# Output projection of a hybrid decoder layer from seven products per 2x2 by 2x2 tiles, with two weight sums made by accumulating DMAs

## The chip, the cores and the metric

One Trainium2 chip, one of its cores. The metric is the device time of one execution in microseconds (us); lower is better. The kernel before took 2497.19 us, the median of 3 runs (2496.21 to 2499.42).

## The reference, cut to what matters

One layer of a decoder trunk on 256 tokens of width 4096: a gated linear attention and a sliding-window attention side by side, gated and merged, one output projection with a residual add, and a final norm. All data are float32.

```python
h = rms_norm(x, norm_gains)
z = h @ w_in                       # 4096 x 19472, split into the parts below
o_a = rms_norm(gla_mix(gq, gk, gv, log_a), gla_norm_gains)
y_a = (o_a * silu(gg)) @ w_gla_out
o_b = swa_sink_mix(sq, sk, sv, sinks)
y_b = (o_b * silu(sg)) @ w_swa_out
merged = sigmoid(ga + b_gates[0]) * y_a + sigmoid(gb + b_gates[1]) * y_b
x = x + merged @ w_out             # 256 x 4096 by 4096 x 4096: what the change is about
out = rms_norm(x, final_norm_gain)
```

## The kernel before

All large projections go through one helper, `gemm` (L125). It makes 512 columns of output for both tiles of 128 tokens, over k tiles of 128 rows. A chunk of two k tiles of weights (128 x 1024, 512 KB) is loaded into `raw` (four buffers), and split in two parts in the format fp32r: ScalarE casts it to `hi` (L154), VectorE subtracts this from `raw` to get `lo` (L155). Each pair of tiles then takes three products, high by high, high by low and low by high (L136 to L138), which add up in one bank of PSUM. The split tiles have three buffers (`STG`). The loads and the split stand in a `tc.high_priority(PRIO)` block, so they are put ahead of other work of their engines.

The program is written with a tile framework: a tile of a pool has as many buffers as `bufs` says, per tag. A new tile of the tag waits until the last reader of the tile that held the buffer is done. The framework orders the instructions of each engine ahead of time from their priorities and from when they could start, so neighbours in the code can change places; each engine then runs its own list in order.

The stages follow one another: the input's norm, the linear attention (two groups of four heads), the window attention, then for each of eight blocks of 512 columns the two gates `ga` and `gb` and the projection `yb` with the merge into `ya` (L502 to L524), and last the output projection. For this the merged activations are transposed and split into `mT` by `transpose_split` (L179), called from `merged` (L499): the first seven blocks before the last `yb` products, the eighth inside the first block of the output projection. The output projection (L530 to L548) then calls `gemm` for each of eight blocks with `wout`, adds the residual (L545), takes squares for the final norm (L546) and multiplies by the gain (L548). In the last block the second token tile's products come late, so that the first tile's final norm lies beside them. At the end each token tile is scaled and stored in five pieces (L549 to L563).

Of the kernel before, what the change touches and what calls it, by code (L numbers as in the profile page):

```python
# [8 lines left out]
F32 = mybir.dt.float32  # L9
# [5 lines left out]
P = 128  # L15
S = 256
# [30 lines left out]
def trunk_kernel(  # L47
# [20 lines left out]
    big = ctx.enter_context(tc.tile_pool(name="big", bufs=1))  # L68
    stage = ctx.enter_context(tc.tile_pool(name="stage", bufs=STG))
    acc_ps = ctx.enter_context(tc.tile_pool(name="acc_ps", bufs=4, space=bass.MemoryType.PSUM))  # L70
    ps = ctx.enter_context(tc.tile_pool(name="ps", bufs=4, space=bass.MemoryType.PSUM))
# [25 lines left out]
    def first_inputs(gp, ssq):  # L97
        """Loads the input as the first block needs it; its squares add up in ssq."""
# [72 lines left out]
    def split_to(dst, src_ps):  # L171
        """dst[:, ..hi/lo.., :] from a PSUM tile of the same layout less the hi/lo axis."""
# [4 lines left out]
    def transpose_split(oT, kt0, src, nk, name):  # L177
        """src [tokens, t, nk*128] -> oT[:, kt0:kt0+nk, hi/lo, tokens]"""
# [12 lines left out]
    # ================= gated linear attention =================  # L191
    with tc.tile_pool(name="gla", bufs=1) as gp:
# [5 lines left out]
        # per-token scale of the input norm  # L198
# [8 lines left out]
        # low-rank decay input, transposed: rows 0-15 from w's high part, 16-31 from its low part  # L207
# [31 lines left out]
        def headsT(name, acc, scale):  # L239
            """[tokens, 4 heads x 128] in PSUM -> [128, head, token]"""  # L240
# [20 lines left out]
        for g in range(2):  # L261
# [3 lines left out]
            # log decays of the group's heads and their running sums in each chunk  # L265
# [51 lines left out]
            # keys of chunks 0 and 1 as chunks 2 and 3 see them  # L317
# [8 lines left out]
            for p in range(2):  # L326
# [6 lines left out]
                # o = A @ v, a head at a time; A is kept transposed, [key, query]  # L333
# [57 lines left out]
    # ================= sliding-window attention =================  # L391
    late = ctx.enter_context(tc.tile_pool(name="late", bufs=1))
# [105 lines left out]
    # ================= gates and merge =================  # L498
    def merged(n):  # L499
        transpose_split(mT, n * 4, ya[:, :, n * NB : (n + 1) * NB], 4, f"m{n}")  # L500

    with tc.tile_pool(name="mrg", bufs=1) as mp:  # L502
        for n in range(NBLK):
# [22 lines left out]
    # ================= output projection, residual, final norm =================  # L526
    with tc.tile_pool(name="fin", bufs=1) as fp:
        gf = fp.tile([P, DM], F32, name="gf")
        nc.scalar.dma_start(gf, gfin.partition_broadcast(P))
        hold = None  # L530
        x2 = big.tile([P, NT, DM], F32, tag="oT", name="x2")
        st = fp.tile([P, NT, NBLK], F32, name="st")
        for n in range(NBLK):
            cs = slice(n * NB, (n + 1) * NB)
            xt = fp.tile([P, NT, NB], F32, tag="xt", name=f"xt{n}", bufs=2)
            nc.scalar.dma_start(xt, x[:, cs].rearrange("(t p) c -> p t c", p=P))
            if n == NBLK - 1:
                hold = late.tile([P, 4, 2, KW, NB], F32R, tag="ya", name="hold")
# [89 lines left out]
```

## Time and profile before

| What | Value |
|---|---|
| median of 3 runs | 2497.19 us |
| span of the profiled execution | 2494.7 us |
| TensorE (PE) busy | 2469.9 us, 99% |
| VectorE (DVE) busy | 1306.1 us, 52% |
| ScalarE (ACT) busy | 1093.1 us, 44% |
| GpSimd (POOL) busy | 41.4 us, 2% |
| moved by DMA | 474.32 MB, 190 GB/s on average |

The profile is of one execution; its own device time is not on the page apart from the span, which reaches from its first to its last instruction. The median of the runs lies 2.5 us above the span. PE is matrix products, PEld their weight loads, SP the engine that issues the weight loads from HBM. "Idle before, releaser" tells what ended an engine's wait.

### The profile page before, as it was taken

The numbers are of one execution on the slowest core, as the hardware profiler recorded it, in microseconds if no ns is written. First come the engines' busy times: TensorE is split into PE (matmuls) and PEld (weight loads), VectorE is DVE, ScalarE is ACT, GpSimd is POOL, SyncE is SP. The second block draws the span as 40 slices with busy tenths as digits, with TensorE's granted clock in tenths as the row PEclk, the third lists the DMA queues.
The fourth block names the chain that finished last, engine by engine and source line by source line (L and its number), as shares of the span: only waits on it lengthen the run. The fifth ranks groups of instructions, "written<-read, shape, count | busy, mean of one in ns | idle before, by whom it ended". The sixth has DMA issues, their size and how long they took to land.

```text
span 2494.7 us, 28744 instructions
## 1 busy us (share of the span) xinstructions
PE 2469.9 (99%) x11220; PEld 2033.3 (82%) x11220; DVE 1306.1 (52%) x1303; ACT 1093.1 (44%) x1289; POOL 41.4 (2%) x52
## 2 busy tenths in 40 slices
PE   8999999999999999999999999999999999999998
PEld 6788888888888888888888888888888888888886
DVE  8565555545444455555555454555545456544544
ACT  6444444434444444544444444444444444444443
POOL 4000000000000000000000000000000000000000
PEclk9999999999999999999999999999999999999999
DMA  7455555445555545454465556665666555665655
GB/s 258 156 175 188 170 175 195 175 168 188 194 192 195 193 148 193 150 171 166 150 211 199 198 198 197 197 202 197 198 196 198 194 194 177 236 211 203 211 203 186
DMA packets 132985, 474.32 MB, mean 190 GB/s; under 512 B 15056, under 2 KB 15440, under 8 KB 132720
## 3 DMA queue, kind: packets, MB, share of 16 engines
q1 hardware_dynamic: 127584, 461.69, 54.5%
q10 hardware_dynamic: 5264, 10.79, 1.4%
q8 instruction: 88, 1.44, 0.2%
q14 instruction: 49, 0.40, 0.0%
HBM read 468.23 MB, written 4.19 MB: 189 GB/s over the span
## 4 chain that ended last, share of the span: by engine, by line
PE 95%; DVE 2%; issue 1%; ACT 1%; DMA 0%; POOL 0%; SPq 0%; ACTq 0%; POOLq 0%; DVEq 0%
PE ga_a L137 5%; PE ga_a L136 5%; PE gb_a L137 5%; PE gb_a L136 5%; PE ga_a L138 5%; PE gb_a L138 5%; PE o_a L136 5%; PE o_a L137 5%; PE o_a L138 5%; PE sg_a L137 2%; PE sg_a L136 2%; PE sg_a L138 2%; PE sq_a L138 2%; PE sq_a L137 2%; PE ya_a L136 2%; PE ya_a L137 2%
## 5 line engine op out<-in xcount | busy, mean ns | idle before, releaser
L155 DVE TENSOR_TENSOR ga_l<-ga_r,ga_h 128x1024 fp32r<-128x1024 f32 x128 | 156.8, 1225 | 171.6 <-ACT ga_h L154 171.6
L155 DVE TENSOR_TENSOR gb_l<-gb_r,gb_h 128x1024 fp32r<-128x1024 f32 x128 | 156.9, 1225 | 171.1 <-ACT gb_h L154 171.1
L155 DVE TENSOR_TENSOR o_l<-o_r,o_h 128x1024 fp32r<-128x1024 f32 x124 | 152.0, 1225 | 161.4 <-ACT o_h L154 161.3
L154 ACT CAST ga_h<-ga_r 128x1024 fp32r<-128x1024 f32 x128 | 135.2, 1057 | 209.8 <-PE ga_a L138 171.5
L154 ACT CAST gb_h<-gb_r 128x1024 fp32r<-128x1024 f32 x128 | 135.2, 1056 | 204.5 <-PE gb_a L138 159.4
L154 ACT CAST o_h<-o_r 128x1024 fp32r<-128x1024 f32 x124 | 131.0, 1056 | 193.2 <-PE o_a L138 186.2
L138 PE MATMUL ga_a<-ga_h,hT 128*128 128x512 f32 x512 | 199.4, 389 | 0.0
L137 PE MATMUL ga_a<-ga_l,hT 128*128 128x512 f32 x512 | 199.2, 389 | 0.0
L136 PE MATMUL ga_a<-ga_h,hT 128*128 128x512 f32 x512 | 199.2, 389 | 0.0
L138 PE MATMUL gb_a<-gb_h,hT 128*128 128x512 f32 x512 | 199.2, 389 | 0.0
L136 PE MATMUL gb_a<-gb_h,hT 128*128 128x512 f32 x512 | 199.2, 389 | 0.0
L137 PE MATMUL gb_a<-gb_l,hT 128*128 128x512 f32 x512 | 199.2, 389 | 0.0
L138 PE MATMUL o_a<-o_h,mT 128*128 128x512 f32 x496 | 193.0, 389 | 0.0
L137 PE MATMUL o_a<-o_l,mT 128*128 128x512 f32 x496 | 193.0, 389 | 0.0
L136 PE MATMUL o_a<-o_h,mT 128*128 128x512 f32 x496 | 192.9, 389 | 0.0
L155 DVE TENSOR_TENSOR ya_l<-ya_r,ya_h 128x1024 fp32r<-128x1024 f32 x64 | 78.4, 1226 | 95.6 <-ACT ya_h L154 95.6
L155 DVE TENSOR_TENSOR sq_l<-sq_r,sq_h 128x1024 fp32r<-128x1024 f32 x64 | 78.4, 1225 | 84.8 <-ACT sq_h L154 84.8
L155 DVE TENSOR_TENSOR yb_l<-yb_r,yb_h 128x1024 fp32r<-128x1024 f32 x64 | 78.4, 1225 | 82.8 <-ACT yb_h L154 82.8
L155 DVE TENSOR_TENSOR gg_l<-gg_r,gg_h 128x1024 fp32r<-128x1024 f32 x64 | 78.3, 1224 | 75.9 <-ACT gg_h L154 75.9
L155 DVE TENSOR_TENSOR sg_l<-sg_r,sg_h 128x1024 fp32r<-128x1024 f32 x64 | 78.3, 1223 | 72.7 <-ACT sg_h L154 72.7
L154 ACT CAST sg_h<-sg_r 128x1024 fp32r<-128x1024 f32 x64 | 67.4, 1053 | 111.0 <-PE sg_a L138 94.7
L155 DVE TENSOR_TENSOR gv_l<-gv_r,gv_h 128x1024 fp32r<-128x1024 f32 x64 | 78.2, 1224 | 67.9 <-ACT gv_h L154 67.9
(278 smaller groups left out, 5568.3 us busy)
## 6 DMA issues: line engine op xcount, KB each, us to landing
ga_r<-in_win_dram SPq DMA_DIRECT2D x128, 512.0 KB, 4.3
gb_r<-in_win_dram SPq DMA_DIRECT2D x128, 512.0 KB, 4.2
o_r<-in_wout_dram SPq DMA_DIRECT2D x128, 512.0 KB, 3.3
gv_r<-in_win_dram SPq DMA_DIRECT2D x64, 512.0 KB, 3.2
gg_r<-in_win_dram SPq DMA_DIRECT2D x64, 512.0 KB, 3.3
ya_r<-in_wgla_dram SPq DMA_DIRECT2D x64, 512.0 KB, 3.2
sq_r<-in_win_dram SPq DMA_DIRECT2D x64, 512.0 KB, 3.2
sg_r<-in_win_dram SPq DMA_DIRECT2D x64, 512.0 KB, 3.3
```

The source lines that it names most:

```text
L136: nc.tensor.matmul(acc[t], lh, hi[:, i, :], start=kt == 0, stop=False)
L137: nc.tensor.matmul(acc[t], lh, lo[:, i, :], start=False, stop=False)
L138: nc.tensor.matmul(acc[t], ll, hi[:, i, :], start=False, stop=kt == nkt - 1)
L154: nc.scalar.copy(hi, raw)
L155: nc.vector.tensor_tensor(lo, raw, hi.bitcast(F32), ALU.subtract)
```

## The change

The output projection no longer goes through `gemm`. Its 2 token tiles, 2 k tiles and 2 column blocks at a time are multiplied with seven products in place of eight, from sums and differences of the tiles (the Winograd form of Strassen's scheme). The left-hand sums are made once by `combine`, for 16 pairs of k tiles. The weights come as four tiles of 128 x 512 in one load of 1 MB (`raw`, two buffers); the host lays them out in that order (`_quads`). Two products take their weight tile and their activations as plain float32 (`right[1]`, `right[2]`). The other five are split as before, one of them from a weight tile itself and four from sums. Two of these sums, `t13`, are made by VectorE in one instruction; the third and the fourth come from adding `raw[:, 0]` and then `raw[:, 3]` into `t13[:, 1]` in place, by DMAs that GpSimd issues with `accum_op`. The split tiles have one buffer each. Seven PSUM banks hold the seven products over all 16 steps, and eight operations then put the four output blocks together from them (`u`, `v`, `y`, `w`). The pools of the earlier stages are closed before this stage, and the new pools take their place; each tile in them waits for what used its own place. `gfin` is loaded in pieces of 1024 columns, and the last block's late second half with `hold` is gone; the stores are four pieces of 1024 columns for each token tile.

```diff
+NFULL = 2
+T13 = 3
+BUFS = {"b": 1, "13": 1, "2": 1, "4": 1}
...
-            if n == NBLK - 1:
-                mT = big.tile([P, KT, 2, S], F32R, tag="hT", name="mT")
-                for m in range(n):
-                    merged(m)
...
+    early.close()
+    NPR = KT // 2
...
+    def combine(j):
+
+        fl, sp_ = full[j // GRP][:, j % GRP], split[j // GRP][:, j % GRP]
+        tp = qps.tile([P, 512], F32, tag="tp", name=f"m_t{j}")
+        for k in range(2):
             for t in range(NT):
...
+                c = (2 * j + k) * P
+                nc.tensor.transpose(tp[:, k * S + t * P : k * S + (t + 1) * P], ya[:, t, c : c + P], ident)
+        tv = tp.rearrange("p (k t c) -> p k t c", k=2, t=NT)
+        cs = fp.tile([P, 6, P], F32, tag="cs", name=f"cs{j}", bufs=2)
+        nc.scalar.copy(fl[:, 0:2, :], tv[:, :, 0, :])
+        nc.scalar.copy(cs[:, 0:2, :], tv[:, :, 1, :])
+        s4 = fl[:, 2, :] if NFULL > 2 else cs[:, 5, :]
+        nc.vector.tensor_tensor(cs[:, 2, :], cs[:, 0, :], cs[:, 1, :], ALU.subtract)
+        nc.vector.tensor_tensor(cs[:, 4, :], fl[:, 0, :], cs[:, 0, :], ALU.subtract)
+        nc.vector.tensor_tensor(cs[:, 3, :], cs[:, 2, :], fl[:, 0, :], ALU.subtract)
+        nc.vector.tensor_tensor(s4, fl[:, 1, :], cs[:, 3, :], ALU.add)
+        c = cs[:, 1 : 8 - NFULL, :]
+        nc.scalar.copy(sp_[:, :, 0, :], c)
+        nc.vector.tensor_tensor(sp_[:, :, 1, :], c, sp_[:, :, 0, :].bitcast(F32), ALU.subtract)
...
+    def sevens(name, w, npr):
+
+        q = {i: qps.tile([P, NB], F32, tag=f"q{i}", name=f"{name}_q{i}") for i in range(1, 8)}
+        for j in range(npr):
+            with tc.high_priority(PRIO):
+                raw = wp.tile([P, 4, NB], F32, tag="raw", name=f"{name}_r{j}", bufs=2)
+                nc.sync.dma_start(raw, w[j])
+                t13 = wp.tile([P, 2, NB], F32, tag="t13", name=f"{name}_t{j}", bufs=T13)
+                nc.vector.tensor_tensor(
+                    t13, raw[:, 0:2, :], raw[:, 2:3, :].broadcast_to([P, 2, NB]), ALU.add
+                )
+
+                def parts(tag, src, n):
+                    hi = wp.tile([P, n, NB], F32R, tag=f"h{tag}", name=f"{name}_h{tag}_{j}", bufs=BUFS[tag])
+                    lo = wp.tile([P, n, NB], F32R, tag=f"l{tag}", name=f"{name}_l{tag}_{j}", bufs=BUFS[tag])
+                    nc.scalar.copy(hi, src)
+                    nc.vector.tensor_tensor(lo, src, hi.bitcast(F32), ALU.subtract)
+                    return [(hi[:, i, :], lo[:, i, :]) for i in range(n)]
+
+                right = {1: raw[:, 0, :], 2: raw[:, 3, :]}
...
+                    right[3], = parts("b", raw[:, 1:2, :], 1)
+                right[5], right[7] = parts("13", t13, 2)
+                t = t13[:, 1, :]
+                nc.gpsimd.dma_start(t, raw[:, 0, :], accum_op=ALU.add)
+                right[6], = parts("2", t13[:, 1:2, :], 1)
+                nc.gpsimd.dma_start(t, raw[:, 3, :], accum_op=ALU.add)
+                right[4], = parts("4", t13[:, 1:2, :], 1)
+            order = (1, 6, 5, 3, 2, 7, 4) if j == npr - 1 else (1, 2, 3, 5, 7, 6, 4)
+            st, sp_ = j == 0, j == npr - 1
+            for i in order:
+                if isinstance(right[i], tuple):
+                    l = split[j // GRP][:, j % GRP, SPLIT[i]]
+                    hi, lo = right[i]
+                    nc.tensor.matmul(q[i], l[:, 0, :], hi, start=st, stop=False)
+                    nc.tensor.matmul(q[i], l[:, 0, :], lo, start=False, stop=False)
+                    nc.tensor.matmul(q[i], l[:, 1, :], hi, start=False, stop=sp_)
+                else:
+                    nc.tensor.matmul(q[i], full[j // GRP][:, j % GRP, FULL[i], :], right[i], start=st, stop=sp_)
+        return q
...
+    for j in range(NPR):
+        combine(j)
+    for n in range(0, NBLK, 2):
...
+        q = sevens(f"o{n}", wout[n // 2], NPR)
...
+        def done(t, i):
+            o, xi = x2[:, t, cs[i]], xt[:, t, i * NB : (i + 1) * NB]
+            add(o, o, xi)
+            nc.scalar.activation(xi, o, AF.Square, accum_out=st[:, t, n + i : n + i + 1])
+            add(o, o, gf_[:, i * NB : (i + 1) * NB], ALU.mult)
+
+        nc.scalar.copy(u, q[1])
+        add(v, q[6], u)
+        add(y, q[5], v, ALU.subtract)
+        add(x2[:, 0, cs[1]], q[3], y)
+        add(x2[:, 0, cs[0]], q[2], u)
+        add(w, q[7], v)
+        add(x2[:, 1, cs[1]], q[5], w, ALU.subtract)
+        add(x2[:, 1, cs[0]], q[4], w)
+        for t, i in ((0, 1), (0, 0), (1, 1), (1, 0)):
+            done(t, i)
```

## Rows read from the trace of the kernel before

**Rows 1.** The page: busy time by engine, and the chain that ended last.
```profile
PE 2469.9 (99%) x11220; PEld 2033.3 (82%) x11220; DVE 1306.1 (52%) x1303; ACT 1093.1 (44%) x1289; POOL 41.4 (2%) x52
...
PE 95%; DVE 2%; issue 1%; ACT 1%; DMA 0%; POOL 0%; SPq 0%; ACTq 0%; POOLq 0%; DVEq 0%
```

**Rows 2.** Busy time by engine in one stretch, the output projection; clock, DMA share, GB/s.
```profile
2134.50:2484.00 349.50, 349.50 (x1546) 289.13 (x1545) 177.44 (x167) 145.42 (x160) 0.55 (x1) 1.00 0.60 208
```

**Rows 3.** Waits from 2140 to 2484 us: us in total, times, longest.
```profile
ACT o_h L154 <- PE o_a L138: 184.5, 116, 2.1
...
ACT o_h L154 <- DMA o_r<-in_wout_dram: 1.6, 3, 0.9
```

**Rows 4.** Timeline of PE near 2300 us: start, duration, engine, line.
```profile
2299.81 0.39 PE L137 MATMUL o_a<-o_l,mT 128*128 128x512 f32 x1
...
2300.49 0.39 PE L137 MATMUL o_a<-o_l,mT 128*128 128x512 f32 x1
```

**Rows 5.** Timeline at the stage's start and at its end.
```profile
2127.90 1.23 DVE L155 TENSOR_TENSOR yb_l<-yb_r,yb_h 128x1024 fp32r<-128x1024 f32 x1 [1.49 <-ACT yb_h L154]
...
2134.48 1.28 DVE L523 TENSOR_TENSOR sgm<-yb_a,sgm 128x512 f32<-128x512 f32 x2
...
2484.06 0.69 DVE L545 TENSOR_TENSOR x<-o_a,xt 128x512 f32<-128x512 f32 x1 [4.98 <-PE o_a L138]
```

**Rows 6.** Timeline of PE, plain float32 products of 256 columns.
```profile
262.41 0.59 PE L366 MATMUL op<-v,ats 128*128 128x256 f32 x2
262.84 0.59 PE L367 MATMUL op<-v,ats 128*128 128x256 f32 x2
```

**Rows 7.** VectorE by line and shape: busy us, mean ns of one.
```profile
L155 DVE TENSOR_TENSOR o_l<-o_r,o_h 128x1024 fp32r<-128x1024 f32 x124 | 152.0, 1225 | 161.4 <-ACT o_h L154 161.3
...
L388 DVE TENSOR_TENSOR gt<-oraw,gt 128x256 f32<-128x256 f32 x16 | 6.2, 420 | 0.2
...
L155 DVE TENSOR_TENSOR gq_l<-gq_r,gq_h 128x512 fp32r<-128x512 f32 x2 | 1.4, 689 | 1.1 <-ACT gq_h L154 1.1
...
L456 DVE TENSOR_TENSOR mx<-mx,sink_sb 128x8 f32<-128x8 f32 x8 | 1.3, 163 | 0.1
```

**Rows 8.** ScalarE by line and shape.
```profile
L154 ACT CAST o_h<-o_r 128x1024 fp32r<-128x1024 f32 x124 | 131.0, 1056 | 193.2 <-PE o_a L138 186.2 <-PE yb_a L138 5.0 <-DMA o_r<-in_wout_dram 1.6
...
L154 ACT CAST gq_h<-gq_r 128x512 fp32r<-128x512 f32 x2 | 1.2, 618 | 0.9 <-DMA gq_r<-in_win_dram 0.9
```

**Rows 9.** DMA issues: count, KB each, median us to landing.
```profile
o_r<-in_wout_dram SPq DMA_DIRECT2D x128, 512.0 KB, 3.3
...
xsb<-in_xT_dram SPq DMA_DIRECT2D x7, 512.0 KB, 6.7
...
gf<-in_gfin_dram ACTq DMA_DIRECT2D x1, 2048.0 KB, 8.1
```

**Rows 10.** The tile `bt`, 256 KB from HBM: 16 loads.
```profile
DMA to landing us min/median/max: 3.9/4.6/6.4
```

**Rows 11.** The output's stores out of SBUF, 256 or 512 KB: 10 stores.
```profile
DMA to landing us min/median/max: 2.1/3.9/4.8
```

**Rows 12.** Timeline of PE: transposes that stand earlier in the code between `yb` products.
```profile
2109.65 0.39 PE L136 MATMUL yb_a<-yb_h,obT 128*128 128x512 f32 x1
...
2110.08 0.66 PE L184 MATMUL m_t<-ident,ya 128*128 128x128 f32 x4
...
2110.49 0.48 PE L137 MATMUL yb_a<-yb_l,obT 128*128 128x512 f32 x1
```

**Rows 13.** Busy time by engine after the last product; the clock stands after POOL's.
```profile
2484.00:2494.70 10.70, 0.02 (x1) 0.00 (x0) 2.82 (x6) 2.91 (x4) 0.56 (x1) 0.63 0.57 223
```

More of the change, by code (lines that the diff above doesn't have):

```diff
@@ L67, in trunk_kernel @@
     const = ctx.enter_context(tc.tile_pool(name="const", bufs=1))
[L68 to L71, printed above, removed]
+    early = ExitStack()
+    big = early.enter_context(tc.tile_pool(name="big", bufs=1))
+    stage = early.enter_context(tc.tile_pool(name="stage", bufs=STG))
+    acc_ps = early.enter_context(tc.tile_pool(name="acc_ps", bufs=4, space=bass.MemoryType.PSUM))
+    ps = early.enter_context(tc.tile_pool(name="ps", bufs=4, space=bass.MemoryType.PSUM))
     def pst(name):
@@ L389, in trunk_kernel @@
                 transpose_split(oaT, pi * 4, gt, 4, f"oa{pi}")
-    late = ctx.enter_context(tc.tile_pool(name="late", bufs=1))
+    late = ctx.enter_context(tc.tile_pool(name="late", bufs=1, side="right"))
     ya = late.tile([P, NT, DM], F32, tag="ya", name="ya")
@@ new lines, in trunk_kernel @@
+    early.close()
+    NPR = KT // 2
+    hp = ctx.enter_context(tc.tile_pool(name="hp", bufs=1, reuse_waits="tile"))
+    wp = ctx.enter_context(tc.tile_pool(name="wp", bufs=1, reuse_waits="tile"))
+    fp = ctx.enter_context(tc.tile_pool(name="fp", bufs=1, reuse_waits="tile"))
+    qps = ctx.enter_context(
+        tc.tile_pool(name="qps", bufs=1, space=bass.MemoryType.PSUM, reuse_waits="tile")
+    )
+    GRP = 4
+    full = [hp.tile([P, GRP, NFULL, P], F32, name=f"full{g}") for g in range(NPR // GRP)]
@@ new lines, in trunk_kernel @@
+    split = [hp.tile([P, GRP, 7 - NFULL, 2, P], F32R, name=f"split{g}") for g in range(NPR // GRP)]
+    def combine(j):
+        fl, sp_ = full[j // GRP][:, j % GRP], split[j // GRP][:, j % GRP]
+        tp = qps.tile([P, 512], F32, tag="tp", name=f"m_t{j}")
+        for k in range(2):
+            for t in range(NT):
+                c = (2 * j + k) * P
[12 more added lines that the diff above has]
+        nc.vector.tensor_tensor(sp_[:, :, 1, :], c, sp_[:, :, 0, :].bitcast(F32), ALU.subtract)
@@ new lines, in trunk_kernel, with add @@
+    x2 = late.tile([P, NT, DM], F32, tag="ya", name="x2")
+    st = fp.tile([P, NT, NBLK], F32, name="st")
+    for j in range(NPR):
+        combine(j)
+    for n in range(0, NBLK, 2):
+        gf_ = fp.tile([P, 2 * NB], F32, tag="gf", name=f"gf{n}")
+        nc.scalar.dma_start(gf_, gfin[n * NB : (n + 2) * NB].partition_broadcast(P))
+        xt = fp.tile([P, NT, 2 * NB], F32, tag="xt", name=f"xt{n}")
+        nc.scalar.dma_start(xt, x[:, n * NB : (n + 2) * NB].rearrange("(t p) c -> p t c", p=P))
+        q = sevens(f"o{n}", wout[n // 2], NPR)
+        cs = [slice((n + i) * NB, (n + i + 1) * NB) for i in range(2)]
+        u = fp.tile([P, NB], F32, tag="u", name=f"u{n}")
+        v = fp.tile([P, NB], F32, tag="v", name=f"v{n}")
+        y = fp.tile([P, NB], F32, tag="y", name=f"y{n}")
+        w = fp.tile([P, NB], F32, tag="w", name=f"w{n}")
+        def add(o, a, b, op=ALU.add):
+            nc.vector.tensor_tensor(o, a, b, op)
+        def done(t, i):
[13 more added lines that the diff above has]
+            done(t, i)
@@ new lines, in trunk_kernel @@
+    for t in range(NT):
+        sf = fp.tile([P, 1], F32, name=f"sf{t}")
+        nc.vector.tensor_reduce(sf, st[:, t, :], AX.X, ALU.add)
+        rms_scale(sf, sf, DM)
+        for c in range(4):
+            os = slice(c * 1024, (c + 1) * 1024)
+            if c % 2 == 0:
+                nc.vector.tensor_scalar(x2[:, t, os], x2[:, t, os], sf, None, ALU.mult)
+            else:
+                nc.scalar.activation(x2[:, t, os], x2[:, t, os], AF.Copy, scale=sf)
+            nc.sync.dma_start(out[t * P : (t + 1) * P, os], x2[:, t, os])
@@ L572, in _tiles, with _quads @@
     return np.ascontiguousarray(w.transpose(3, 0, 2, 1, 4))
+def _quads(w, nblk):
+    import numpy as np
+    w = w.reshape(w.shape[0] // (2 * P), 2, P, nblk // 2, 2, NB)
+    return np.stack([w[:, k, :, :, n] for k, n in ((0, 0), (1, 1), (0, 1), (1, 0))], 3).transpose(2, 0, 1, 3, 4).copy()
 def kernel(**inputs):
```

44 lines of the change are left out of this document (6 added, 38 removed).

## The prediction

> **What bounds the kernel now.** I read the page first. TensorE (PE) is busy 99% of the span and carries 95% of the chain that ended last, the DMA 0% [rows 1]. So what the change is worth has to be read in the stage that it rewrites. The output projection runs from the end of the last `yb` products at 2134.5 us to 2484 us; the table by stretches shows PE busy in all 349.5 us of it, VectorE (DVE) in 177 and ScalarE (ACT) in 145, at the full granted clock, with the DMA engines 60% busy [rows 2]. The waits of the same stretch say who waits for whom: the split of the weights waits for PE to give a staging buffer back (184.5 us), and for its own data from HBM only 1.6 us [rows 3]. The weights are thus always ready before PE asks for them. Between two starts of the same line lie 0.68 us for three products of 512 columns, 0.227 us each [rows 4]; the 1536 of the stage give 348 us. After the last product comes a tail of 10.6 us: add, squares, scale, store [rows 5].
>
> The span is 2494.7 us; the median of the runs, 2497.19, lies 2.5 us above it. I count in the span and add 2.5.
>
> **What PE gains.** For each pair of k tiles and pair of column blocks there are now 8 products in three parts, 24 x 0.227 = 5.44 us. After, there are 7: five in three parts and two as plain float32. The trace has plain float32 products in the attention parts: each is recorded as two instructions, and for 256 columns the next pair starts 0.43 us later [rows 6]. At 512 columns that is twice as much, 0.86 us (lower bound 0.43, if most of it were a fixed cost; no row suggests more than double). One step is 15 x 0.227 + 2 x 0.86 = 5.12 us, and 64 steps (4 pairs of column blocks x 16 pairs of k tiles) are 328 us: PE itself gains 20 us.
>
> **What the other engines get.** Durations of DVE: 1.225 us for 1024 columns, 0.689 for 512, 0.42 for 256, 0.163 for nearly nothing; ACT casts: 1.056 and 0.618 [rows 7, 8]. A step asks of DVE the pair of sums `t13` (1.225), the low part of `t13` (1.225) and three low parts of 512 (2.07): 4.52 us, against 2.45 for the two chunks that it replaces. ACT has 1.056 + 3 x 0.618 = 2.91 us. At each of four column pairs DVE has 15 adds and multiplies of 512 columns, 10.3 us. The 16 `combine` calls have four subtractions of 128 columns (about 0.28 each, between the 0.163 and the 0.42) and one of 640 (about 0.82), 1.94 us, so 31 us. DVE's sum is 289 + 41 + 31 = 361 us: more than the 349.5 us that the stage takes today, before any wait is counted.
>
> **The new chain, and why it decides.** One weight tile `raw` (1 MB) has two buffers. Its last reader is the second accumulating DMA, which adds `raw[:,3]` into the running sum. The steps ahead of that stand in one line, because each rewrites what the one before had to read: load; `t13` sum; cast and low part of `t13` (both must have read it); first accumulate into it; cast and low part of that ("2"); second accumulate. Only then may the load of the step after next start. Before, a raw buffer was free as soon as DVE had made the low part, and there were four.
>
> Priced: the load is 1 MB. Loads of 512 KB land 3.3 us after issue, the one of 2048 KB 8.1 [rows 9]; 1.6 per 512 KB gives 4.9. Then 1.225 + 1.056 + 1.225, and 0.618 + 0.689 for "2". Without the accumulates the chain is 9.71 us. An accumulate X within SBUF, issued from GpSimd (POOL), is in no row. It moves 256 KB as 128 rows of 2 KB; the nearest row has that size and shape, the load `bt`, which lands after 3.9 to 6.4 us with a median of 4.6 beside weight loads [rows 10]. That is a read from HBM and no addition. Bound below: the quickest store, out of SBUF, took 2.1 us [rows 11]. Bound above: 6.4, the slowest `bt`. It can cost nothing only if nothing waited for it, which the chain excludes. I take 4.6. The chain is 9.71 + 9.2 = 18.9 us, and with two buffers two steps pass in it: 9.46 us a step against PE's 5.12. For 64 steps that is 605 us. With 2.1 us it would be 13.9 us a pair and 445 us; with 6.4, 22.5 and 720.
>
> The Trainium skill (page "DMA: Bandwidth & Descriptors", section "Anatomy of one DMA — SWDGE (gpsimd) path") fits a DMA issued from GpSimd as 2.0 us plus bytes over 436 GB/s. By that an accumulate would take 2.6 us (an estimate from the page), the chain 14.9 us and the 64 steps 477 us. The `bt` row is nearly twice that figure for the same bytes. No run here shows an accumulate yet.
>
> A second loop runs beside the first, because the split tiles `h13`, `l13`, `h2`, `l2`, `h4`, `l4` have one buffer each. If PE keeps the order of the code, product 7 of a step must end before the next `t13` cast starts, and product 4 of that next step is the last link before further products: 1.06 + 1.23 + X + 1.31 + X + 1.31 + 0.7 + 3.8 (the products of the following step up to 7) = 9.4 + 2X for two steps, 18.6 us. It is as long as the first, so mixing up PE's order would not help much. The order need not be kept: today transposes from earlier in the code stand between later products where their buffers were late [rows 12].
>
> **Queues.** POOL has no other work in the stage (0.55 us, rows 2) and issues both accumulates of a step in one queue; a waiting one holds back only accumulates behind it. On DVE the low part of "2" waits for an accumulate, and sums, low parts of the next step and the adds of a column pair may stand behind it; what that costs lies within the two buffers' slack of one DVE instruction or two, and I count nothing for it in the middle, up to 3.7 us a pair of steps at the top of the range. SP issues only the weight loads, and each waits for the second accumulate of two steps back; nothing but the stores at the end is behind them.
>
> **Start, boundaries, end.** The first load can go where the last `yb` chunk has left the staging area, at about 2129.1 us, the end of the row at 2127.90 [rows 5]. The second chain trails the first by 3.6 us, since its `t13` cast waits for product 7 (8.4 + 1.36 - 6.1). The `combine` calls today lie under the `yb` products; now they wait for the freed PSUM banks and stand in the first 31 us of the stage. In a step of 9.46 us their 1.94 us are covered; if the chain were short, they would cost up to 31. At the three inner boundaries DVE's 10.3 us come on top of its 9.0 in a period of 18.9: I count 2 us each (0 to 10). Evacuation of the last column pair begins before the last product, whose order was turned for it, so the end is: cast and low part of "4" 1.3, product 0.7, one more add 0.7, and today's 10.6.
>
> Sum: 2129.1 + 605 + 3.6 + 6 + 13.3 = 2757 us of span, and 2760 with the 2.5.
>
> **The rivals.**
> 1. *The accumulate is quick*, between 2.1 and 3.5 us. The chain is 13.9 to 16.7 us, the time 2600 to 2690. For it: data from SBUF have no HBM behind them, and nothing loads the queue of POOL. Against it: an accumulate reads two operands and its rows are 2 KB.
> 2. *DVE is the bound*, the DMAs cheap or spread better than I see: 361 us, PE idle 33 of them, 2129 + 5 + 361 + 13 + 3 = 2511, up to 2580 if chain and DVE nearly meet. Against it: the chain needs X near 1 us.
> 3. *The clock falls.* With PE at work 5.1 us of 9.5 there are gaps. In the last 10.7 us of the span, where PE has nothing to do, the mean granted clock is 0.63 [rows 13], so part of it at the lower level of 1.2 GHz. At that level a step is 15 x 0.427 + 2 x 1.71 = 9.8 us, more than the chain's 9.46, and 64 steps are 628 us. Products would then end late for the single buffers too: 2780 to 2850, and with accumulates of 6 us and loads of 6.7 (the row of `xsb`, where the DMA was crowded, rows 9) up to 2930. The Trainium skill ("TensorE: Matmul & The Clock Gate", section "Why this matters for your kernels") tells to avoid idle gaps between bursts, since the array then returns to half clock; the row of the tail agrees.
> 4. *The steps don't overlap at all*, since the in-order queues got the low part of "4" ahead of the next step's sums: 15.3 us a step, 982 us, about 3130. Rows 12 speak against it.
> 5. *Faster:* PE stays the bound. The place is the raw buffer: if its return took less than two PE steps (10.24 us), the 20 us would be gained, and 2477 to 2490 come out. The deciding point is 9.71 + 2X below 10.24, X below 0.3 us, and DVE's `combine` work under the `yb` products. Every row of a transfer is seven times that.
> 6. *It doesn't do what it says:* float32 products of 512 columns cost more than 1.13 us, so that PE has no gain. It changes little while the chain decides.
>
> **How the numbers follow.** The main case with X of about 3.5 to 5.5 (2690 to 2830) has 0.60, the quick accumulate 0.14, clock and crowded transfers (2830 to 2930) 0.14, no overlap 0.04, DVE 0.05, faster 0.02, no change 0.01. The predicted time is that of the main case, 2760 us. The range is 2600 to 2920: below it lie DVE, no change and faster, above it no overlap and part of the crowded case, together under 0.2. A measurement tells 0.2% from no change. Faster 0.02, the same 0.02, slower 0.96.
>
> **What would show it.** Right: loads of `raw` waiting on SP for the second accumulate (not for PE or DVE); a period of about 18.9 us per two steps; accumulates landing after 4 to 5 us; PE busy about 55% of the stage, with its waits on "4" and "2". The terms one by one: float32 pairs 0.86 us apart, loads near 4.9 us, DVE 4.5 us a step. Wrong: PE busy throughout, a stage below 350 us, accumulates below 1 us, or SP waiting for PE, which would make the products and not the chain the bound.

## The result and the profile after

The changed kernel takes 2918.77 us (median of three, 2917.49 to 2920.57) against 2497.19: 1.1688 times as long, 95% interval 1.1667 to 1.1709. That is 421.6 us more, where 263 were forecast. The sign, the place and what the loads wait for came out as predicted; 159 us are missing from the sum. The time lies 1 us below the upper end of the range, and in the stretch that the prediction gave to the clock and crowded transfers (2830 to 2930, chance 0.14), not in that of its main case. That it lies within the range is luck: the upper end was made with accumulates of 6 us and loads of 6.7, and the terms below are others.

The page of the kernel after, busy time by engine and the chain that ended last (for [rows 1]):

```profile
PE 2612.1 (90%) x10900; PEld 2017.0 (69%) x10900; DVE 1460.5 (50%) x1587; ACT 1150.9 (39%) x1453; POOL 152.8 (5%) x180
...
PE 70%; issue 13%; DMA 12%; DVE 2%; POOL 1%; ACT 1%; SPq 0%; POOLq 0%; ACTq 0%; DVEq 0%
```

Before, the chain ran through PE for 95% of the span and through DMAs for none of it; now DMAs hold 12% of 2917 us, 350 us ("issue" is time for which the profile shows no wait). The stretches of the output projection and of its tail, with the columns of [rows 2] (length, busy PE, PEld, DVE, ACT, POOL, clock, DMA share, GB/s):

```profile
2135.00:2898.00 763.00, 493.49 (x1272) 274.40 (x1271) 337.73 (x449) 208.58 (x329) 111.06 (x128) 0.74 0.54 137
2898.00:2917.00 19.00, 0.01 (x1) 0.00 (x0) 7.36 (x15) 6.21 (x10) 1.39 (x2) 0.51 0.56 221
```

The stage has grown from 349.5 to 763 us, and no engine fills it: PE is busy 65%, at a mean clock of 0.74, DVE 44%. The tail, 10.7 us in [rows 13], is 19. The queue of the weight loads (SP) from 2135 to 2898 us, waits with total, times, longest:

```profile
SPq L569 <- DMA o_t<-o_r: 720.0, 62, 22.6
```

62 of 64 loads wait, all for an accumulate and none for PE (for [rows 3]). One period of two steps, from the timeline (start, duration, engine, line, operation, idle before and its releaser). L571 is the pair of sums, L578 a cast, L579 a low part, L589 the first accumulate and L591 the second, L599 to L601 the parts of a split product, L603 a plain one:

```profile
2612.69 0.62 ACT L578 CAST o_h<-o_t 128x512 fp32r<-128x512 f32 x1 [6.72 <-DMA o_t<-o_r]
...
2613.36 0.80 PE L599 MATMUL o_q<-o_h,split 128*128 128x512 f32 x1 [5.26 <-ACT o_h L578]
...
2613.95 1.22 DVE L571 TENSOR_TENSOR o_t<-o_r 128x1024 f32<-128x1024 f32 x1
...
2615.11 3.51 PE L603 MATMUL o_q<-o_r,full 128*128 128x512 f32 x4
...
2617.55 1.22 DVE L571 TENSOR_TENSOR o_t<-o_r 128x1024 f32<-128x1024 f32 x1
...
2617.80 0.86 POOL L589 DMA_DIRECT2D o_t<-o_r  x1 [11.19 <-DMA o_r<-in_wout_dram]
...
2621.63 1.57 ACT L578 CAST o_h<-o_t 128x1024 fp32r<-128x1024 f32 x2 [1.67 <-PE o_q L601]
...
2624.23 0.86 POOL L589 DMA_DIRECT2D o_t<-o_r  x1 [5.57 <-DVE o_l L579]
2624.83 1.15 POOL L591 DMA_DIRECT2D o_t<-o_r  x1
2627.69 0.62 ACT L578 CAST o_h<-o_t 128x512 fp32r<-128x512 f32 x1 [4.49 <-DMA o_t<-o_r]
2629.08 0.62 ACT L578 CAST o_h<-o_t 128x512 fp32r<-128x512 f32 x1 [0.77 <-DMA o_t<-o_r]
2629.32 0.86 POOL L591 DMA_DIRECT2D o_t<-o_r  x1 [3.35 <-DVE o_l L579]
2636.46 0.62 ACT L578 CAST o_h<-o_t 128x512 fp32r<-128x512 f32 x1 [6.75 <-DMA o_t<-o_r]
2637.72 1.22 DVE L571 TENSOR_TENSOR o_t<-o_r 128x1024 f32<-128x1024 f32 x1
2641.57 1.23 DVE L571 TENSOR_TENSOR o_t<-o_r 128x1024 f32<-128x1024 f32 x1 [0.30 <-DMA o_r<-in_wout_dram]
```

The sums of the even step stand at 2613.95 and 2637.72, those of the odd one at 2617.55 and 2641.57. Follow the odd step: sums at 2617.55; its cast not before 2621.63; first accumulate issued at 2624.23, used at 2627.69; second issued at 2629.32, used at 2636.46; the load that this sets free is used at 2641.57. That is 24.0 us for two steps. Over the whole stage the loads were issued from 2125.2 to 2875.9 us, 31 such periods of 24.2. The same two DMA issues of 2629 to 2630 us, with KB each and us to landing:

```profile
o_r<-in_wout_dram SPq DMA_DIRECT2D x1, 1024.0 KB, 5.6
o_t<-o_r POOLq DMA_DIRECT2D x1, 256.0 KB, 7.0
```

And the accumulate issued at 2617.80, with no load under way (2617 to 2618 us):

```profile
o_t<-o_r POOLq DMA_DIRECT2D x1, 256.0 KB, 3.3
```

An accumulate by itself lands after 3.3 us; the one that is issued within 0.2 us of a 1 MB load after 7.0. From 2200 to 2600 us the first accumulates land after 3.2 to 4.2 us (median 3.3), the second ones of the even steps mostly after 4.2, 0.6 us behind a first one, and those of the odd steps after 6.8 to 7.1. At the boundaries between column pairs, beside the loads of `xt` and `gf` as well, it is 9.9 to 10.9.

What the DMA engines move meanwhile is in the trace too. By queue, with packets, MB and the share of 16 engines, from 2629 to 2634 us and then to 2636.5 (q1 carries the load, q0 the accumulate):

```profile
q1 hardware_dynamic: 113, 0.93, 70.3%
...
q0 software_dynamic: 144, 0.26, 57.8%
q1 hardware_dynamic: 31, 0.12, 11.9%
```

Up to 2634 us not one packet of the accumulate has moved, 4.7 us after its issue; all 144 lie at the end of the load and behind it. GpSimd's own part of the issue ends at 2630.2, and DVE is idle from 2630.4 to 2637.1 us, so neither of these engines holds it up. Of the accumulate issued at 2617.80 all 144 lie between 2619.2 and 2621 us.

### The profile page after: what moved, and what is told of

Read it like the earlier page. It is cut to its first block, busy times and chain, and to the rows that moved or that the text cites. A ratio compares the mean times of both kernels' runs of the same rounds, so it can differ in the third digit from the quotient of the medians.

```text
span 2917.0 us, 28776 instructions
## 1 busy us (share of the span) xinstructions
PE 2612.1 (90%) x10900; PEld 2017.0 (69%) x10900; DVE 1460.5 (50%) x1587; ACT 1150.9 (39%) x1453; POOL 152.8 (5%) x180
## 4 chain that ended last, share of the span: by engine, by line
PE 70%; issue 13%; DMA 12%; DVE 2%; POOL 1%; ACT 1%; SPq 0%; POOLq 0%; ACTq 0%; DVEq 0%
DMA o_t<-o_r 6%; DMA o_r<-in_wout_dram 6%; PE ga_a L142 4%; PE ga_a L140 4%; PE gb_a L142 4%; PE gb_a L140 4%; PE ga_a L141 4%; PE gb_a L141 4%; PE sg_a L141 2%; PE sg_a L140 2%; PE sg_a L142 2%; PE sq_a L140 2%; PE sq_a L142 2%; PE ya_a L140 2%; PE ya_a L141 2%
## 5 line engine op out<-in xcount | busy, mean ns | idle before, releaser
L579 DVE TENSOR_TENSOR o_l<-o_t,o_h 128x512 fp32r<-128x512 f32 (+1 forms) x192 | 164.4, 868 | 353.0 <-ACT o_h L578 352.9
L599 PE MATMUL o_q<-o_h,split 128*128 128x512 f32 x256 | 121.2, 527 | 234.5 <-ACT o_h L578 234.5
L578 ACT CAST o_h<-o_t 128x512 fp32r<-128x512 f32 (+1 forms) x192 | 143.3, 760 | 433.6 <-DMA o_t<-o_r 348.2
L599 PEld LDWEIGHTS o_q<-o_h,split 128*128 128x128 f32 x256 | 54.8, 216 | 292.7 <-ACT o_h L578 285.0
L159 DVE TENSOR_TENSOR ga_l<-ga_r,ga_h 128x1024 fp32r<-128x1024 f32 x128 | 156.8, 1225 | 171.6 <-ACT ga_h L158 171.6
L159 DVE TENSOR_TENSOR gb_l<-gb_r,gb_h 128x1024 fp32r<-128x1024 f32 x128 | 156.8, 1225 | 171.2 <-ACT gb_h L158 171.2
L603 PE MATMUL o_q<-o_r,full 128*128 128x512 f32 x256 | 172.7, 788 | 23.5 <-DMA o_r<-in_wout_dram 23.5
L589 POOL DMA_DIRECT2D o_t<-o_r x64 | 55.3, 864 | 2079.3 <-DVE o_l L579 1968.6
L600 PE MATMUL o_q<-o_l,split 128*128 128x512 f32 x256 | 145.7, 586 | 9.5 <-DVE o_l L579 8.9
L159 DVE TENSOR_TENSOR ya_l<-ya_r,ya_h 128x1024 fp32r<-128x1024 f32 x64 | 78.4, 1225 | 95.7 <-ACT ya_h L158 95.7
L159 DVE TENSOR_TENSOR yb_l<-yb_r,yb_h 128x1024 fp32r<-128x1024 f32 x64 | 78.4, 1225 | 85.1 <-ACT yb_h L158 85.1
L159 DVE TENSOR_TENSOR sq_l<-sq_r,sq_h 128x1024 fp32r<-128x1024 f32 x64 | 78.4, 1225 | 84.8 <-ACT sq_h L158 84.8
L601 PE MATMUL o_q<-o_h,split 128*128 128x512 f32 x256 | 117.1, 475 | 0.0
```

The lines of the kernel that those rows point to most:

```text
L159: nc.vector.tensor_tensor(lo, raw, hi.bitcast(F32), ALU.subtract)
L578: nc.scalar.copy(hi, src)
L579: nc.vector.tensor_tensor(lo, src, hi.bitcast(F32), ALU.subtract)
L589: nc.gpsimd.dma_start(t, raw[:, 0, :], accum_op=ALU.add)
L599: nc.tensor.matmul(q[i], l[:, 0, :], hi, start=st, stop=False)
L600: nc.tensor.matmul(q[i], l[:, 0, :], lo, start=False, stop=False)
```

## Experiments

My theory (the *buffer theory*): two raw buffers are held to the end of a chain of two accumulates, so accumulates and their contention with loads (both under way at once) set the pace. Rivals: the *clock theory* (PE at the lower clock is itself the bound) and the *queue theory* (the in-order lists of DVE, ACT and POOL, with single split buffers, are the bound, and the number of raw buffers is not). "Period" below is the distance from the first load to the last over 31, as above: 24.2 us in the changed kernel.

**1. No accumulates.**

```diff
-                nc.gpsimd.dma_start(t, raw[:, 0, :], accum_op=ALU.add)
                 right[6], = parts("2", t13[:, 1:2, :], 1)
-                nc.gpsimd.dma_start(t, raw[:, 3, :], accum_op=ALU.add)
```

> Leaves out both accumulating DMAs, so products 6 and 4 use an unfinished sum; everything else stays. After the change a pair of steps takes 24.0 us. Buffer theory (two raw buffers that are held until the second accumulate has landed set the pace): the chain loses both transfers, raw is free after the split, a step falls to 5.2 to 6 us (VectorE 4.5, TensorE 5.1), the time to 2500 to 2560 us. Clock theory (TensorE at the lower clock with single split buffers sets the pace, 9.8 us a step): the time stays above 2700 us.

2507.55 us, 1.0042 times before (1.0022 to 1.0062). The accumulates and what they trigger are thus 411 of the 421.6 us, and the clock theory as a bound of its own falls. Its stretches, columns as above:

```profile
2130.00:2260.00 130.00, 123.82 (x474) 82.17 (x473) 125.97 (x206) 81.68 (x144) 0.00 (x0) 0.99 0.52 186
2260.00:2480.00 220.00, 217.20 (x794) 147.82 (x793) 193.35 (x242) 120.33 (x189) 0.00 (x0) 1.00 0.59 217
2484.00:2505.40 21.40, 0.22 (x1) 0.00 (x0) 9.87 (x20) 6.94 (x12) 1.38 (x2) 0.57 0.50 196
```

PE is back at the full clock and busy 99% of the second stretch. A step of it, by PE's timeline (lines behind the accumulates are two lower in this kernel):

```profile
2299.89 0.79 PE L597 MATMUL o_q<-o_hb,split 128*128 128x512 f32 x1
...
2303.74 1.88 PE L601 MATMUL o_q<-o_r,full 128*128 128x512 f32 x4
2305.05 0.79 PE L597 MATMUL o_q<-o_hb,split 128*128 128x512 f32 x1
```

A step is 5.16 us (predicted 5.12), 330 for the 64. Still the kernel is not faster than before: in the first stretch DVE is busy 126 of 130 us with `combine` beside the sums and low parts, and the tail is 21 us in place of 10.7. With the sums for nothing, this change comes out 0.4% slower.

**2. Three raw buffers.** To make room, `cs` has one.

```diff
-                raw = wp.tile([P, 4, NB], F32, tag="raw", name=f"{name}_r{j}", bufs=2)
+                raw = wp.tile([P, 4, NB], F32, tag="raw", name=f"{name}_r{j}", bufs=3)
```

> Three raw buffers in place of two (the room comes from one cs buffer in the start of the stage). Buffer theory: three steps instead of two pass in about 24 us, 8 us a step, 64 x 4 = 256 us less, 2620 to 2720 us. Queue theory (the low part of sum 4 of the odd step stands ahead of the next pair's sums in the in-order lists, and this locks the steps in pairs): the pair stays at 22 to 24 us, above 2850 us. Clock theory: at least 9.8 us a step, 2780 us or more.

2711.39 us, 1.0859 (1.0828 to 1.0891): 207 us come back through one buffer more, within the buffer theory's range. The queue theory as a bound by itself falls. But the framework makes the lists anew for three buffers, and their order is another one: in the changed kernel DVE makes the sums of both steps of a pair ahead of the four low parts behind their accumulates, here sums and these low parts alternate. How much of the gain is the buffer and how much the order is not shown; the loads still wait 516 us in all for accumulates.

**3. Two buffers for `h13` and `l13`.** To make room, `cs` has one.

```diff
-BUFS = {"b": 1, "13": 1, "2": 1, "4": 1}
+BUFS = {"b": 1, "13": 2, "2": 1, "4": 1}
```

> Two buffers for the split tiles of t13 (the room comes from one cs buffer). The odd step's cast of t13 now waits about 2.9 us per pair for products of the even step. Buffer theory with this wait as a term of the chain: 32 x 2.9 = 93 us less, about 2825 us. Queue theory: the even step's sums still stand behind the odd step's last low part, the wait moves there, less than 40 us of gain, above 2880 us.

2873.86 us, 1.151 (1.1477 to 1.1543), 45 us less; period 22.8. Neither figure was met. By this kernel's timeline the odd step's `t13` cast starts 1.9 us after its sums (2407.54 to 2409.47) and not 4.1 (2617.55 to 2621.63), and in every other pair about 3; it still stands behind the cast of `hb`. Its second accumulate meets a load as before: issued at 2417.16 us, used at 2424.59, 7.4 us. The single split buffer is a part of the cost, not the larger one.

**4. Half a load.**

```diff
-                nc.sync.dma_start(raw, w[j])
+                nc.sync.dma_start(raw, w[j][:, 0:2, :])
...
```

> Half of each weight load is left out: two of the four tiles come from one tile loaded once, so the output is not the projection; 512 KB per step are loaded, instructions and accumulates stay. In the kernel after, the even step's second accumulate lands in 4.2 us and the odd one's in 7.1 us, which starts with the next 1 MB load. Contention theory: the load is 2 us shorter and the odd accumulate falls to about 5 us, 4 us per pair, 32 x 4 = 128 us less, about 2790 us. Without contention only the load's 2 us count: 64 us less, about 2855 us, the odd accumulate still 7 us.

2813.49 us, 1.1268 (1.1235 to 1.1301), 105 less; period 20.9. By the timeline of this kernel the second accumulate of an odd step, beside a load of 512 KB:

```profile
2432.79 0.86 POOL L591 DMA_DIRECT2D o_t<-o_r  x1 [3.36 <-DVE o_l L579]
...
2438.55 1.56 ACT L578 CAST o_h<-o_t 128x512 fp32r<-128x512 f32 x2 [5.37 <-DMA o_t<-o_r]
```

5.8 us from issue to use, against 7.1 (2629.32 to 2636.46) beside 1 MB. The accumulate is slower the more load stands ahead of it. The time lies between the two figures, nearer to that of the contention theory (2790).

**5. Product 4 in plain float32.** No cast and no low part behind the second accumulate.

```diff
-                right[4], = parts("4", t13[:, 1:2, :], 1)
+                right[4] = t13[:, 1, :]
...
```

> Product 4 takes its sum as plain float32, with a left-hand tile that stands in for the right one, so its result is not the projection's; cast and low part of sum 4 fall away, and with them the last instructions of ScalarE and VectorE that wait for the second accumulate. Accumulates, loads and buffers stay. Queue theory: in the kernel after, the even step's sums stand about 3 us behind the odd step's low part of 4, which delays products 5 and 7 and so the odd step's cast (2.9 us a pair); without it a pair takes 21 us instead of 24, 2820 to 2840 us. If the in-order lists don't matter beside the buffers, the time stays at 2900 to 2920 us.

2845.37 us, 1.1393 (1.136 to 1.1426), 73 less, just above the queue theory's figure. But it doesn't prove what it was made for, since the gain is not the instructions taken out: the run falls into stretches of different kinds. From 2376.6 to 2448.1 us its loads come 17.9 us apart for two steps, from 2509.1 to 2632.0 us 24.6. The landings of its first accumulates (L589), from 2376 to 2448 us and then from 2509 to 2632:

```profile
DMA to landing us min/median/max: 3.4/3.6/3.9
...
DMA to landing us min/median/max: 6.8/6.9/7.6
```

The median of the second ones is 3.3 in both. In the slow stretch every first accumulate is issued within about 0.3 us of a load, in the quick one 2.3 us or more behind it. In the slow one ACT stands 8.5 us in each step at the cast behind that accumulate, two neighbouring steps of the timeline:

```profile
2602.38 0.62 ACT L578 CAST o_h<-o_t 128x512 fp32r<-128x512 f32 x1 [8.53 <-DMA o_t<-o_r]
...
2614.82 0.62 ACT L578 CAST o_h<-o_t 128x512 fp32r<-128x512 f32 x1 [8.81 <-DMA o_t<-o_r]
```

The same instructions with the same buffers thus take a quarter less time in one stretch than in the other. The order of the lists differs between the two: in the slow one DVE, ACT and POOL end one step's work before the next step's begins, in the quick one the sums of a pair's second step stand ahead of the low parts behind the first step's accumulates. So the in-order lists matter; how much of the 6.7 us is the meeting and how much the overlap lost is not parted.

**6. The sums by GpSimd's own addition, in place.**

```diff
-                nc.gpsimd.dma_start(t, raw[:, 0, :], accum_op=ALU.add)
+                nc.gpsimd.tensor_tensor(t, t, raw[:, 0, :], ALU.add)
```

The same for `raw[:, 3, :]`.

> Both sums by GpSimd additions in place, no accumulating DMA. A GpSimd addition of 512 columns took 1.68 us in the trace of before (the squares of the input). Buffer theory: the chain is 4.9 + 3.5 + 1.7 + 1.3 + 1.7 = 13.1 us, 6.5 us a step, about 2575 us; with the wait of the odd cast left in, 8 us a step, 2660 us. Theory that the transfers alone made the loss and buffers don't matter: about 2508 us, as with both left out.

2690.93 us, 1.0775 (1.0743 to 1.0806): all three figures missed, the nearest, 2660 with the wait of the odd cast, by 31 us. Groups of lines from 2200 to 2600 us (busy, mean ns):

```profile
L589 POOL TENSOR_TENSOR o_t<-o_t,o_r 128x512 f32<-128x512 f32 x48 | 88.0, 1833 | 167.1 <-DVE o_l L579 167.1
L579 DVE TENSOR_TENSOR o_l<-o_t,o_h 128x1024 fp32r<-128x1024 f32 x48 | 70.3, 1464 | 21.6 <-ACT o_h L578 21.6
```

DVE's subtraction of 1024 columns, 1225 ns in [rows 7], takes 1464 beside an adding GpSimd; I had left it at its old price.

**7. The same, out of place, into tiles of their own.**

```diff
+                s2 = wp.tile([P, 1, NB], F32, tag="s2", name=f"{name}_s2_{j}", bufs=2)
+                s4 = wp.tile([P, 1, NB], F32, tag="s4", name=f"{name}_s4_{j}", bufs=2)
+                nc.gpsimd.tensor_tensor(s2, t13[:, 1:2, :], raw[:, 0:1, :], ALU.add)
+                nc.gpsimd.tensor_tensor(s4, s2, raw[:, 3:4, :], ALU.add)
...
```

> Both sums by GpSimd into tiles of their own (two buffers each, t13 has two instead of three), so the sums needn't wait for cast and low part. Buffer theory: raw is held for 4.9 + 1.2 + 3.4 = 9.5 us, 4.75 us a step, less than TensorE's 5.16; TensorE and VectorE set the pace as with both sums left out, 2505 to 2530 us. If GpSimd's additions slow VectorE on their shared memory port, VectorE's 1024 column subtraction grows beyond 1.23 us and the time beyond 2560 us.

2617.21 us, 1.0479 (1.0449 to 1.051); the second expectation holds. The stretch from 2270 to 2450 us, and its groups:

```profile
2270.00:2450.00 180.00, 152.73 (x504) 92.52 (x504) 166.92 (x158) 80.11 (x123) 91.27 (x52) 0.98 0.47 169
```

```profile
L579 DVE TENSOR_TENSOR o_l<-o_s,o_h 128x512 fp32r<-128x512 f32 x52 | 55.0, 1073 | 6.5 <-ACT o_h L578 4.8
L592 POOL TENSOR_TENSOR o_s<-o_s,o_r 128x512 f32<-128x512 f32 x26 | 47.4, 1823 | 2.0
...
L579 DVE TENSOR_TENSOR o_l<-o_t,o_h 128x1024 fp32r<-128x1024 f32 x27 | 43.7, 1620 | 6.8 <-ACT o_h L578 6.8
```

The chain is gone and DVE is the bound, busy 167 of 180 us, because its subtractions take 1073 and 1620 ns, not 689 and 1225. The Trainium skill ("SBUF — State Buffer", section "SBUF: two separate sides") says why such a pair can't run side by side: VectorE and GpSimd share a port pair that one instruction locks whole, also a VectorE operation with two SBUF inputs against a GpSimd operation that reads SBUF. The lengthened rows agree; no run here shows the lock itself.

**8. The sums by VectorE, in place.**

```diff
-                nc.gpsimd.dma_start(t, raw[:, 0, :], accum_op=ALU.add)
+                nc.vector.tensor_tensor(t, t, raw[:, 0, :], ALU.add)
```

The same for `raw[:, 3, :]`.

> Both sums by VectorE additions in place (0.69 us each). VectorE has 4.52 + 1.38 = 5.9 us a step, 378 us in 64 steps and 450 with the start and the column pairs. The chain is 4.9 + 3.5 + 0.7 + 1.3 + 0.7 = 11.1 us, 5.55 us a step. VectorE sets the pace: 2580 to 2600 us. If waits in order add to it, up to 2640 us.

2616.54 us, 1.0477 (1.0443 to 1.0511), in the upper part of what was expected (2580 to 2640). From 2200 to 2600 us:

```profile
2200.00:2600.00 400.00, 343.49 (x1062) 190.16 (x1060) 343.72 (x468) 171.00 (x261) 0.00 (x0) 0.97 0.42 154
```

Two more instructions a step on DVE cost less than two accumulates, by 302 us. PE and DVE are each busy 86%: neither is full, and the waits of the stretch are spread over casts, low parts and loads, none above 75 us.

**9. Copies in place of accumulates.**

```diff
-                nc.gpsimd.dma_start(t, raw[:, 0, :], accum_op=ALU.add)
+                nc.gpsimd.dma_start(t, raw[:, 0, :])
```

The same for `raw[:, 3, :]`.

> Both DMAs stay, on the same queue and in the same place, but copy instead of adding, so the sums are wrong. Theory that the price of an accumulate is that of any such transfer (fixed part, and the queue behind the weight load): landing stays at 3.4 to 3.8 us, 7 beside a load, and the time at 2900 to 2920 us. Theory that the addition, which has to read its destination too, costs: copies land about 1 us sooner each, 2850 us or less.

2826.06 us, 1.1319 (1.1296 to 1.1341), 93 less, as the second theory has it. DMA issues of this kernel from 2200 to 2600 us:

```profile
o_t<-o_r POOLq DMA_DIRECT2D x76, 256.0 KB, 2.5
```

The median of the accumulates is 3.7, but both medians mix transfers by themselves and beside loads. Of the first ones alone, which meet no load, it is 2.3 here and 3.3 in the changed kernel: an accumulate costs 1.0 us more than a copy. Beside a load the copy takes 5.3 (issued at 2418.53, used at 2423.83 on its timeline): contention is not particular to accumulates. DVE, ACT and POOL keep the order of their lists in this run, and away from the boundaries two steps take 20.4 us against 23.8: 3.4 less, where the two landings of an odd step are 2.8 shorter together.

**10. Half the columns of each accumulate.**

```diff
-                nc.gpsimd.dma_start(t, raw[:, 0, :], accum_op=ALU.add)
+                nc.gpsimd.dma_start(t[:, 0:NB // 2], raw[:, 0, 0 : NB // 2], accum_op=ALU.add)
```

The same for `raw[:, 3, :]`.

> Each accumulate takes 256 of the 512 columns, so half of each sum is left unfinished. If the price goes with bytes: 3.4 us falls to about 2.7 and the 7 us beside a load to about 4.5, 3.5 us a pair, about 2805 us. If it is fixed: 3.4 stays above 3.1 and 7 above 6.3, less than 40 us of gain, 2880 us or more. Packets of 1 KB in place of 2 KB may take as long as before; that would look like the second.

2748.05 us, 1.1006 (1.0984 to 1.1028), 171 less, better than both figures. Its accumulates, from 2200 to 2600 us:

```profile
o_t<-o_r POOLq DMA_DIRECT2D x87, 128.0 KB, 2.7
```

By itself an accumulate of half the bytes takes 2.7 us and not 3.3. But not all of the gain is the bytes: this run too falls into two kinds of stretches. A second accumulate (L591) issued 0.7 us behind a load at 2257.00 us, and its load:

```profile
o_r<-in_wout_dram SPq DMA_DIRECT2D x1, 1024.0 KB, 5.0
o_t<-o_r POOLq DMA_DIRECT2D x1, 128.0 KB, 5.0
```

There, from 2235.5 to 2297.3 us, the lists have the order of the changed kernel, and two steps take 20.6 us. From 2376.0 to 2459.3 us they have another order: the second accumulates are issued 2.8 us or more behind a load, land after 2.6 to 2.9, and two steps take 16.7. Half the bytes beside a load thus still take 5.0 us, and the time of the whole run decides between neither of the two figures expected.

**11. Only the second sum on VectorE.**

```diff
-                nc.gpsimd.dma_start(t, raw[:, 3, :], accum_op=ALU.add)
+                nc.vector.tensor_tensor(t, t, raw[:, 3, :], ALU.add)
```

> The second sum by VectorE in place (0.69 us), the first stays an accumulating DMA. VectorE has 5.2 us a step. If the buffer chain is right and the 7 us belong to the accumulate that starts with a load, the chain loses at least 3.4 and at most 6.4 us: 18 to 21 us a pair, 2705 to 2800 us; at the upper end if the first accumulate now collides with the other step's load. If both accumulates cost alike, 3.5 us: 2815 us.

2740.06 us, 1.0974 (1.0952 to 1.0996), as expected. One accumulate in place of two gives 179 us back; the other is worth 124 (run 8).

**12. No accumulates, and the subtractions of `combine` on GpSimd.**

```diff
-        nc.vector.tensor_tensor(cs[:, 2, :], cs[:, 0, :], cs[:, 1, :], ALU.subtract)
+        nc.gpsimd.tensor_tensor(cs[:, 2, :], cs[:, 0, :], cs[:, 1, :], ALU.subtract)
```

The same for the other three.

> Leaves out both accumulates, as in the first experiment (2507.5 us), and gives the four subtractions of combine to GpSimd. In that experiment VectorE was busy 126 of the 130 us from 2130 to 2260 us. If VectorE's work in the start is the floor, 64 x 0.28 = 18 us go from it and 10 to 18 us from the time: 2490 to 2498 us, the level of the kernel before. If the start is bound by the chain of transposes and copies, or GpSimd slows VectorE, it stays at 2503 to 2512 us.

2530.05 us, 1.0134 (1.0117 to 1.0151): a miss, 22 us slower than run 1. From 2130 to 2260 us:

```profile
2130.00:2260.00 130.00, 109.14 (x386) 71.50 (x385) 97.91 (x113) 66.32 (x118) 49.30 (x64) 0.92 0.42 149
...
L554 POOL TENSOR_TENSOR cs<-cs,full 128x128 f32<-128x128 f32 x16 | 16.4, 1025 | 0.0
...
ACT split L557 <- POOL cs L555: 37.8, 15, 3.9
```

DVE is relieved, 98 us in place of 126, but PE is busy 109 in place of 124: a subtraction of 285 ns on DVE takes up to 1025 on GpSimd, in a row with transposes and copies, and ACT's copy at the end of that row waits 37.8 of the 130 us for GpSimd. That this row now decides is likely and not shown by a run. So the DVE limit at the start of run 1 is read from its row and not proven.

## Why the prediction was right in kind and short by 159 us

Right were these steps. SP waits for the second accumulate alone. The number of raw buffers matters (run 2, with the reserve made there). PE's step is 5.16 us against 5.12, and two plain products of 512 columns are recorded in 1.88 us at full clock. The rival with DVE as the bound at 2511, for cheap sums, is met in its number by run 1 (2507.55) and not in kind: from 2260 to 2480 us PE is busy 99% there and DVE 88%. A load takes 5.1 us here, against 4.9. PE is busy 65% of the stage and not 55%, since a part of its products runs at the lower clock. The rival of a quick accumulate (2600 to 2690) had its price right for an accumulate by itself and its time wrong, by the two terms below. Of steps that don't overlap (3130) nothing is seen in the pairs above. In the sixth rival the price at which PE gains nothing is 1.02 us by its own terms (9 x 0.227, halved) and not 1.13; nothing rests on it.

The span, counted in the same four pieces as predicted and as measured:

| | predicted | measured | difference |
|---|---|---|---|
| first load issued | 2129.1 | 2125.2 | -3.9 |
| to the last load, 31 periods (predicted 18.9 each, and 6 for the boundaries) | 592.0 | 750.7 | +158.7 |
| last load to last product | 24.5 | 22.1 | -2.4 |
| tail | 11.3 | 19.0 | +7.7 |
| span | 2756.9 | 2917.0 | +160.1 |

The miss is the period. Its terms, for the odd step above:

| | predicted | measured |
|---|---|---|
| load, issue to use | 4.9 | 5.1 |
| pair of sums | 1.2 | 1.2 |
| wait for the split buffers `hb`, `h13` | 0 | 2.9 |
| cast and low part of `t13` | 2.3 | 2.6 |
| first accumulate | 4.6 | 3.5 |
| cast and low part of "2" | 1.3 | 1.6 |
| second accumulate | 4.6 | 7.1 |
| sum | 18.9 | 24.0 |

Of the 5.1 us that are missing the wait is 2.9 and the two accumulates together 1.4. A loop with a wait in it is not the one that holds the period. For the even step it is the same: its load, issued at 2629.5 us, lands after 5.6, and its sums start 2.6 us later, at 2637.72. The loop without a wait is the second one of the prediction, through the single split buffers in PE's order, which it put at 18.6 us and called as long as the first. From the odd step's second accumulate, used at 2612.69, to the next, used at 2636.46:

| | predicted | measured |
|---|---|---|
| cast of "4", product 4, the next step's products up to 7 | 5.8 | 8.9 |
| cast and low part of `t13` | 2.3 | 2.6 |
| first accumulate | 4.6 | 3.5 |
| cast and low part of "2" | 1.3 | 1.6 |
| second accumulate | 4.6 | 7.1 |
| sum | 18.6 | 23.8 |

The two loops share the accumulates. Why a third raw buffer helps all the same is not shown in detail; its run has other lists.

**The step that failed** is "I take 4.6" for an accumulate, one price for both. The first is cheaper than that and the second much dearer, because the second accumulate of the even step frees its buffer: SP's load leaves at once, and the odd step's second accumulate goes out within 0.2 us of it. The nearest row, `bt` beside weight loads [rows 10], held both cases in its spread of 3.9 to 6.4; I took its middle and asked of neither accumulate which load would be under way. Runs 4 and 9 show it: the second accumulate takes 5.8 us beside a smaller load, and a copy 5.3. In runs 5 and 10 one and the same kernel takes 24.6 us for two steps where an accumulate meets a load and 17.9 where none does, or 20.6 and 16.7; but the lists have another order there too, so this is not the meeting alone. By the rows of the queues above the accumulate's data move only at the end of the load's; why is open. For a transfer by itself the figure of the Trainium skill that the prediction cites, 2.6 us, is nearer to the copies (median 2.3, run 9) than to the accumulates (3.3).

**The second failure** is "I count nothing for it in the middle, up to 3.7 us a pair of steps at the top of the range", for waits in the in-order lists. It is 2.9 us, the largest term of the miss. The odd step's cast waits for PE to leave the single split buffers, and PE is late twice over: the even step's products start behind "4" of the step before, which waits for the slow accumulate, and PE has stood idle 5.3 us ahead of it (at 2613.36), after which the two plain products take 3.51 us, not 1.88. So the clock rival was partly true, as 1.6 of these 2.9 us by that difference, which is an estimate: no run parts the clock from the order. Run 3 took the wait for `h13` away and gained 1.4 us a period.

**The tail** was put at today's 10.6 us. In the kernel before, the first token tile is scaled and stored while PE still works. The last lines of its timeline, and then those of the kernel after:

```profile
2479.71 10.92 SPq L563 DMA_DIRECT2D out_dram<-x  x8
...
2484.06 0.69 DVE L545 TENSOR_TENSOR x<-o_a,xt 128x512 f32<-128x512 f32 x1 [4.98 <-PE o_a L138]
```

```profile
2897.62 0.40 PE L601 MATMUL o_q<-o_h,split 128*128 128x512 f32 x1
...
2904.08 7.90 SPq L651 DMA_DIRECT2D out_dram<-x  x8
```

There the stores begin 4.3 us before the last add. Seven products that each feed several output blocks end together, so both token tiles' adds, squares and stores come behind the last product: 6.5 us from the start of the last product to the first store, and 8 us more in all than [rows 13]. The diff showed it (the last block's late half is gone), and I had not priced it.

## What to carry to other kernels

A cheaper set of products is worth only what the chain that feeds it leaves: count how many buffers are held till the last link, and divide the whole chain by that number before counting what PE gains. Do the same for every single buffer: the loop that holds the period is the one without a wait in it. Price a DMA in such a chain by what its own completion releases, since the load that it sets free runs beside the next one. Where lists are ordered ahead, look whether an edit, or another stretch of the same run, has them in another order before putting a gain down to one cause. Take a spread in the nearest row as a question about which case each use will meet, not as a middle.

## What the runs showed of the hardware

- An accumulating DMA of 256 KB within SBUF lands after 3.3 us by itself, after 7.0 when it is issued within 0.2 us of a 1 MB load and after 5.7 beside one of 512 KB (run 4); a copy of that size after 2.3 by itself and 5.2 when it is issued 0.8 us behind a 1 MB load (run 9); an accumulate of 128 KB after 2.7 by itself and 5.0 when it is issued 0.7 us behind one (run 10).
- In the meeting at 2629 us the accumulate's packets move at the end of the load's: none in the 4.7 us after its issue (2629.32 to 2634).
- GpSimd's queue is busy 0.86 us at the issue of an accumulate and 0.54 at that of a copy (run 9).
- DVE's subtraction of 1024 columns went from 1225 to 1464 and 1620 ns beside additions on GpSimd, that of 512 from 689 to 1073 (run 7).
- Behind 5.3 us of idle time PE's products stand at the lower of its two levels (1.2 GHz): the mean granted clock is 0.52 from 2613.2 to 2618.6 us. PE is busy in nearly all of that stretch, and from 2618.6 to 2627 us the clock is 1.00 (2.4 GHz) and products of 512 columns are 0.23 us apart.
